# Copying softmax probabilities into float32r tiles by DMA before their transposes, and products of 128 columns in place of tiles of zeros

## The chip, the cores and the metric

The kernel runs on one core of one Trainium2 chip. Its time is the device time in microseconds (us) of one execution; three runs of the kernel before gave a median of 1428.13 us (1425.39 to 1431.31). PE is the matrix engine, DVE the vector engine, ACT the scalar engine, POOL the general-purpose engine, SP the engine that issues most DMAs. All engines run their own lists of instructions in a fixed order and wait for each other through semaphores.

## The reference, cut to what matters

One decoder layer with three branches. The change lies in the two attention branches, which have the same core; branch B is dense and causal:

```
# 8 heads, 1024 queries and keys, blocks of 128 queries
sc = einsum('bqhd,bkhd->bhqk', q, k).astype(float32) * d ** -0.5
sc = where(key_pos <= q_pos, sc, -1e30)
p  = softmax(sc, axis=-1)
o  = einsum('bhqk,bkhd->bqhd', p, v)
```

Branch A has the same products, with a mask that keeps 256 chosen keys for each query. The rest of the layer (norms, the large projections, the choice of the 256 keys, gates, the output projection) is not changed.

## The kernel before, in words

All large products are made from float32r operands: a value x is split into a high part, x copied to a tile of type float32r (which changes its last bits), and a low part, x minus the high part. A product of two split operands is two or three products.

`attention` (quoted at the end of this section) runs over 32 units for each branch: 8 heads, and within a head four pairs of query blocks G in the order 3, 0, 2, 1. A unit has two query blocks, b = 0 and b = 1, with (2G+1)*128 and (2G+2)*128 keys. For each block `Scores.mm` makes the scores on PE (tiles `b_3S`, lines 997 to 999: three products for each stretch of at most 512 keys), `masked` negates them into SBUF and takes the row's extreme on DVE (line 494), `Scores.exp` takes the exponential on ACT (line 513), and `Scores.norm` multiplies by one over the sum on DVE (line 523). The result is the tile `b_3p`: plain float32, queries on partitions, keys along the row.

`PV` then needs the probabilities with the keys on partitions. `PV.pt(kp)` transposes, on PE (line 466, into the PSUM tile `b_3pt`), the 128x128 pieces of two key blocks and two query blocks; ACT copies the four pieces into a float32r tile `th` (line 468), DVE forms the low part `tl` (line 469). `PV.mmv(kp)` makes four products with V (lines 479 and 480, tile `b_3o`): two key blocks, each times `th` and times `tl`, 256 columns wide. In the last pair of key blocks the piece (later keys, earlier queries) is masked entirely. Before, it is a strip of zeros in a fixed tile (`zt`), so that the products keep 256 columns. In the same way a score product for 128 keys is made 256 columns wide (`s_chunks`).

Between these steps PE has other work: `kv_gen` (tiles `kv`) and `k_prep` (`bkt`, line 967) prepare the next heads, `q_prep` (`b_0q`, line 979) transposes the next queries, and `Filler` makes gate products (tile `f`, lines 277 to 279, 128x512), whose weights SP loads in halves (`f_1_0r`, line 393) into a pool of `FW` split tiles. Branch B takes eight column blocks of such filler, 384 products. The code gives an order; a scheduler that plans the whole program then moves instructions of each engine, filler above all, into places where it expects the engine to wait. So the order on each engine is not that of the code, but it is fixed when the kernel is built.

In branch A the queries are already transposed as float32r (line 1465, with the float32r unit matrix `identr`); the probabilities of both branches are transposed as float32 with `ident`.

Heads are numbered 0 to 7 below, and "a G = 3 unit" is the unit with the last 256 queries of a head, the longest one.

Of the kernel before, what the change touches and what calls it, by code (L numbers as in the profile page):

```python
# [21 lines left out]
S = 1024  # L22
# [11 lines left out]
FW = 6  # L34
# [39 lines left out]
ZTB = 2  # L74
PVB = (2, 2)
PVA = (2, 2)
# [33 lines left out]
def hybrid_kernel(  # L110
# [70 lines left out]
    # rotary tables: cos / sin of f32(position) * f32(inv_freq), by token block  # L181
# [40 lines left out]
    # DRAM scratch  # L222
# [30 lines left out]
    def wload(pool, nm, srcs, a, n):  # L253
        """srcs: list of ([128, a, w] DRAM view, w); -> (hi, lo) [P, a, n]"""
# [26 lines left out]
    def proj_w(nm, pool, w, cols, nk, per=None):  # L281
        """cols: list of (c0, n) -> one (hi, lo) for each 128 rows"""
# [9 lines left out]
    def proj(nm, ks, lhs, tbs, chunks, consume):  # L292
        """out[tok, cols]; chunks: list of (off, n) within the columns"""
# [118 lines left out]
    def s_chunks(n):  # L412
        """(first key, width of the product, width used) of each bank"""
        if n <= 512:
            return [(0, max(n, 256), n)]
# [17 lines left out]
    zt = []  # L433
    zcount = [0]
    pv_bufs = [2, 2]

    def zero_tiles(wk, n):
        zt[:] = [[wk.tile([P, 4, P], FR, name=f"zt{i}{j}", bufs=1) for j in range(2)] for i in range(n)]
        for t2 in zt:
            for t in t2:  # L440
                nc.gpsimd.memset(t[:, 0, :].bitcast(F32), 0.0)

    class PV:
        """P of two query blocks (2G, 2G + 1) times V, transposed; vst(kt): [128, 128], high and low
        parts of V, the high part where the head's rows of the result lie."""

        def __init__(self, nm, wk, G, sc, hh, vst, o_dst, done):
            self.nm, self.wk, self.nk, self.Pt, self.vst, self.o_dst, self.done = nm, wk, G + 1, sc.Pt, vst, o_dst, done
            self.hh = hh
# [3 lines left out]
        def pt(self, kp):  # L453
            nm, wk, Pt = self.nm, self.wk, self.Pt
            tp = ps_t(f"{nm}pt{kp}").rearrange("p (a c) -> p a c", a=4)
            last = kp == self.nk - 1
            if last:
                th, tl = zt[zcount[0] % len(zt)]
                zcount[0] += 1
                order = [(1, 2 * kp + 1, 1), (2, 2 * kp, 0), (3, 2 * kp, 1)]  # L460
            else:
                th = wk.tile([P, 4, P], FR, tag="pth", name=f"{nm}th{kp}", bufs=pv_bufs[0])
                tl = wk.tile([P, 4, P], FR, tag="ptl", name=f"{nm}tl{kp}", bufs=pv_bufs[0])
                order = [(2 * a + b, 2 * kp + a, b) for a in range(2) for b in range(2)]
# [5 lines left out]
            kts = (2 * kp + 1, 2 * kp) if last else (2 * kp, 2 * kp + 1)  # L470
            self.t[kp] = (th.rearrange("p (a b) c -> p a (b c)", a=2), tl.rearrange("p (a b) c -> p a (b c)", a=2), kts)

        def mmv(self, kp):
            if self.o2 is None:
                self.o2 = ps_mm(f"{self.nm}o2")
            th, tl, kts = self.t.pop(kp)
# [15 lines left out]
    def masked(pt, sp, m, mask, k0, mx, c):  # L492
        """-(scores + mask), and its least value"""
# [8 lines left out]
    class Scores:  # L502
        def __init__(self, nm, wk, G, mm):
            self.nm, self.wk, self.G, self._mm = nm, wk, G, mm
            self.rs = sm.tile([P, 2], F32, tag="rsb", name=nm + "rs")
            self.Pt = []
# [10 lines left out]
        def norm(self):  # L517
            ri = sm.tile([P, 2], F32, tag="rib", name=self.nm + "ri")
            nc.vector.reciprocal(ri, self.rs)
            for b in range(2):  # L520
# [3 lines left out]
                                  scalar2=None, op0=ALU.mult)  # L524

# [3 lines left out]
    def p_tile(wk, G, nm):  # L529
        if G >= 2:  # L530
            return wk.tile([P, S], F32, tag="ptA", name=nm)
        return wk.tile([P, 512], F32, tag="ptB", name=nm)

    def attention(gen, k_prep, q_prep, scores, pv, fill, per, pre, GEN):
        """Head pairs; the next pair's operands are made between the units of this one."""
# [21 lines left out]
        def fl(k):  # L557
            """work of the next pair, then gate products"""
# [54 lines left out]
    # ================= memory branch =================  # L613
# [984 lines left out]
```

## Time and profile before

| | |
|---|---|
| runs of the kernel before | 1428.13 us, median of 3 (1425.39 to 1431.31) |
| the profiled execution | span 1427.6 us from its first to its last instruction |
| PE busy in the span | 1366.2 us (96%) |
| PE weight loads | 1173.0 us (82%) |
| DVE, ACT, POOL | 967.5 us (68%), 687.7 us (48%), 270.2 us (19%) |
| share of the last chain | PE 68%, DVE 15%, ACT 6%, issue 4%, DMA 4% |
| branch B, attention | 285 to 526 us |
| branch A, attention | 955 to 1255 us |

The page gives no other time for the profiled execution than its span. The span lies 0.5 us below the median of the runs. PE bounds most of the kernel: the 40 slices show it at eight or nine tenths nearly everywhere. Matmuls are pipelined and their rows overlap, so what one costs PE is the distance from its start to the next start, not its length.

### The profile page before, as it was taken

The numbers are of one execution on the slowest core, as the hardware profiler recorded it, in microseconds if no ns is written. First come the engines' busy times: TensorE is split into PE (matmuls) and PEld (weight loads), VectorE is DVE, ScalarE is ACT, GpSimd is POOL, SyncE is SP. The second block draws the span as 40 slices with busy tenths as digits, with TensorE's granted clock in tenths as the row PEclk, the third lists the DMA queues.
The fourth block names the chain that finished last, engine by engine and source line by source line (L and its number), as shares of the span: only waits on it lengthen the run. The fifth ranks groups of instructions, "written<-read, shape, count | busy, mean of one in ns | idle before, by whom it ended". The sixth has DMA issues, their size and how long they took to land.

```text
span 1427.6 us, 20798 instructions
## 1 busy us (share of the span) xinstructions
PE 1366.2 (96%) x7440; PEld 1173.0 (82%) x7440; DVE 967.5 (68%) x2409; ACT 687.7 (48%) x1488; POOL 270.2 (19%) x254
## 2 busy tenths in 40 slices
PE   7999999999999999898988998899999999999998
PEld 5998888888888889786867886689899898877887
DVE  5935446678888861479879678777777868836511
ACT  6635433356666651464576563224555535633200
POOL 3150003511102000200232335331202011003200
PEclk9999999999999999999998999999999999999999
DMA  7411222311111120210224325630201001185622
GB/s 245 136 45 52 78 59 86 114 56 41 49 56 53 45 93 20 67 45 23 89 79 151 97 75 182 193 85 9 67 23 45 31 15 45 38 276 184 210 96 74
DMA packets 124631, 122.34 MB, mean 86 GB/s; under 512 B 20336, under 2 KB 90224, under 8 KB 124528
## 3 DMA queue, kind: packets, MB, share of 16 engines
q1 hardware_dynamic: 123952, 118.92, 26.8%
q10 hardware_dynamic: 576, 2.10, 0.4%
q8 instruction: 58, 0.95, 0.3%
q14 instruction: 45, 0.37, 0.1%
HBM read 87.93 MB, written 33.06 MB: 85 GB/s over the span
## 4 chain that ended last, share of the span: by engine, by line
PE 68%; DVE 15%; ACT 6%; issue 4%; DMA 4%; POOL 1%; SPq 1%; ACTq 0%; DVEq 0%; POOLq 0%
PE f L277 5%; PE f L278 5%; PE f L279 4%; DVE kdj L1039 3%; PE a L277 3%; PE a L278 3%; PE a L279 3%; PE o L277 2%; PE o L278 2%; PE o L279 2%; ACT kag L1049 2%; PE br L277 2%; PE br L278 2%; PE br L279 2%; DVE sz L1292 1%
## 5 line engine op out<-in xcount | busy, mean ns | idle before, releaser
L1049 ACT ACTIVATE kag<-idx,kaT 128x512 bf16<-128x512 f32 (+2 forms) x96 | 82.9, 864 | 56.0 <-DVE kaT L1077 39.4
L277 PE MATMUL f<-hTh,f_0h 128*128 128x512 f32 x184 | 77.0, 419 | 1.9 <-ACT f_0h L248 1.2
L277 PE MATMUL f<-hTh,f_1h 128*128 128x512 f32 x184 | 75.6, 411 | 1.3 <-ACT f_1h L248 1.3
L279 PE MATMUL f<-hTh,f_0l 128*128 128x512 f32 x184 | 74.4, 405 | 0.6 <-POOL f_0l L251 0.6
L278 PE MATMUL f<-hTl,f_0h 128*128 128x512 f32 x184 | 74.5, 405 | 0.0
L279 PE MATMUL f<-hTh,f_1l 128*128 128x512 f32 x184 | 74.0, 402 | 0.0
L278 PE MATMUL f<-hTl,f_1h 128*128 128x512 f32 x184 | 73.6, 400 | 0.0
L1568 DVE TENSOR_TENSOR xr<-o,xr 128x512 f32<-128x512 f32 x16 | 11.1, 691 | 64.0 <-PE o L279 64.0
L1223 ACT ACTIVATE irl<-is 128x512 f32<-128x512 f32 (+1 forms) x80 | 37.6, 524 | 24.2 <-DVE idx L1229 15.5
L1526 POOL TENSOR_TENSOR ac<-ac,tg 128x512 f32<-128x512 f32 x16 | 23.5, 1469 | 128.6 <-DMA wo_3r<-in_w_out_dram 109.9
L1039 DVE TENSOR_SCALAR_CACHE_REDUCE kdj<-kdh,kdT 128x384 bf16<-128x384 bf16 (+2 forms) x48 | 46.3, 965 | 0.8
L1039 DVE TENSOR_SCALAR_CACHE_REDUCE kdj<-idx,kdT 128x384 bf16<-128x384 f32 (+2 forms) x48 | 46.2, 963 | 0.6
L369 ACT ACTIVATE fo<-f 128x512 f32<-128x512 f32 x48 | 28.7, 599 | 35.2 <-PE f L279 29.0
L279 PEld LDWEIGHTS f<-hTh,f_0l 128*128 128x128 f32 x184 | 35.2, 191 | 7.9 <-POOL f_0l L251 1.1
L1229 DVE SCALAR_TENSOR_TENSOR idx<-irl,wi,idx 128x1024 f32<-128x1024 f32 (+5 forms) x42 | 40.6, 966 | 1.5 <-ACT irl L1223 0.4
L277 PEld LDWEIGHTS f<-hTh,f_0h 128*128 128x128 f32 x184 | 35.1, 191 | 7.2 <-ACT f_0h L248 1.4
L279 PEld LDWEIGHTS f<-hTh,f_1l 128*128 128x128 f32 x184 | 34.8, 189 | 7.0 <-DVE f_1l L251 0.6
L277 PEld LDWEIGHTS f<-hTh,f_1h 128*128 128x128 f32 x184 | 35.0, 190 | 6.7 <-ACT f_1h L248 2.1
L278 PEld LDWEIGHTS f<-hTl,f_1h 128*128 128x128 f32 x184 | 34.9, 190 | 5.2
L278 PEld LDWEIGHTS f<-hTl,f_0h 128*128 128x128 f32 x184 | 35.3, 192 | 4.3
L1412 ACT ACTIVATE asq<-a 128x256 f32<-128x256 f32 x32 | 12.3, 384 | 51.1 <-PE a L279 50.9
L1266 DVE SCALAR_TENSOR_TENSOR sz<-sz,z 128x512 f32<-128x512 f32 x24 | 16.4, 683 | 27.7 <-ACT sz L1265 27.7
(1215 smaller groups left out, 4862.1 us busy)
## 6 DMA issues: line engine op xcount, KB each, us to landing
s_tg<-fo SPq DMA_DIRECT2D x48, 256.0 KB, 2.0
tg<-s_tg SPq DMA_DIRECT2D x48, 256.0 KB, 3.0
f_0r<-in_w_in_dram SPq DMA_DIRECT2D x23, 256.0 KB, 3.0
f_1r<-in_w_in_dram SPq DMA_DIRECT2D x23, 256.0 KB, 2.9
xx<-in_x_dram SPq DMA_DIRECT2D x8, 512.0 KB, 7.3
osb<-s_o SPq DMA_DIRECT2D x8, 512.0 KB, 3.8
s_acc<-acc SPq DMA_DIRECT2D x16, 256.0 KB, 2.4
ac<-s_acc SPq DMA_DIRECT2D x16, 256.0 KB, 3.4
```

The source lines that it names most:

```text
L277: nc.tensor.matmul(ps, ah, bh, start=start, stop=False)
L278: nc.tensor.matmul(ps, ah, bl, start=False, stop=False)
L279: nc.tensor.matmul(ps, al, bh, start=False, stop=stop)
L369: nc.scalar.activation(o, ps, AF.Tanh, scale=0.5)
L1039: nc.vector.tensor_scalar(out=junk, in0=src[t], scalar1=T[:, i:i + 1], scalar2=0.0, op0=op, op1=ALU.add, accum_out=cnt[:, i:i + 1])
L1049: nc.scalar.activation(junk, idx[t], AF.Sign, bias=T[:, i:i + 1], accum_out=cnt[:, i:i + 1])
L1223: nc.scalar.activation(rl[:, k0:k0 + m], sp[:, 0:m], AF.Relu)
L1229: i_ = nc.vector.scalar_tensor_tensor(out=acc[:, 0:n], in0=rl[:, 0:n], scalar=wc, in1=acc[:, 0:n], op0=ALU.mult, op1=ALU.add)
L1266: zi[0] = nc.vector.scalar_tensor_tensor(out=sz, in0=sz, scalar=1.0, in1=pz[j], op0=ALU.add, op1=ALU.mult)
L1292: i_ = (nc.gpsimd if n and PMUL else nc.vector).tensor_tensor(sz, osb[:, cs], sz, op=ALU.mult)
L1412: nc.scalar.activation(sq.rearrange("p h d -> p (h d)"), ps[:, 0:256], AF.Square)
L1526: nc.gpsimd.tensor_tensor(ac, ac, tg, op=ALU.add)
```

## The change

For branch B alone each normalised tile of probabilities is copied by an SP DMA, SBUF to SBUF, into a second tile whose type is float32r (`b_3r`); the DMA sees both as float32 and moves the words as they are. The transposes then read that tile, with `identr`, into a PSUM tile of type float32r. In both branches the last pair of key blocks has three pieces instead of four, and its second pair of products has 128 columns; the tiles of zeros go, and a score product for 128 keys has 128 columns. To make room, the filler's pool has 5 tiles instead of 6 and branch B's `o2s` one buffer instead of two; branch A's `th` and `tl` have three buffers instead of two. The remaining lines of the diff take comments away.

```diff
-FW = 6
+FW = 5
...
-ZTB = 2
-PVB = (2, 2)
-PVA = (2, 2)
+PVB = (2, 1)
+PVA = (3, 2)
...
         if n <= 512:
-            return [(0, max(n, 256), n)]
+            return [(0, n, n)]
...
         def pt(self, kp):
             nm, wk, Pt = self.nm, self.wk, self.Pt
-            tp = ps_t(f"{nm}pt{kp}").rearrange("p (a c) -> p a c", a=4)
+            Pr = self.Pr
+            tp = ps_t(f"{nm}pt{kp}", FR if Pr else F32).rearrange("p (a c) -> p a c", a=4)
             last = kp == self.nk - 1
-            if last:
-                th, tl = zt[zcount[0] % len(zt)]
-                zcount[0] += 1
-                order = [(1, 2 * kp + 1, 1), (2, 2 * kp, 0), (3, 2 * kp, 1)]
-            else:
...
-            for i, kt, b in order:
-                nc.tensor.transpose(tp[:, i, :], Pt[b][:, kt * P:(kt + 1) * P], ident)
-            v = slice(1 if last else 0, 4)
-            nc.scalar.copy(th[:, v, :], tp[:, v, :])
-            nc.vector.tensor_tensor(tl[:, v, :], tp[:, v, :], f(th[:, v, :]), op=ALU.subtract)
+            th = wk.tile([P, 4, P], FR, tag="pth", name=f"{nm}th{kp}", bufs=pv_bufs[0])
+            tl = wk.tile([P, 4, P], FR, tag="ptl", name=f"{nm}tl{kp}", bufs=pv_bufs[0])
+            order = [(2 * kp + a, b) for a in range(2) for b in range(2) if not (last and a > b)]
+            v = len(order)
+            for i, (kt, b) in enumerate(order):
+                ks = slice(kt * P, (kt + 1) * P)
+                if Pr:
+                    nc.tensor.transpose(tp[:, i, :], Pr[b][:, ks], identr)
+                else:
+                    nc.tensor.transpose(tp[:, i, :], Pt[b][:, ks], ident)
+            tp = f(tp) if Pr else tp
+            nc.scalar.copy(th[:, 0:v, :], tp[:, 0:v, :])
+            nc.vector.tensor_tensor(tl[:, 0:v, :], tp[:, 0:v, :], f(th[:, 0:v, :]), op=ALU.subtract)
...
         def mmv(self, kp):
...
+            last = kp == self.nk - 1
             for a in range(2):
-                vs = self.vst(kts[a])
-                nc.tensor.matmul(self.o2[:, 0:256], vs, th[:, a], start=(kp == 0 and a == 0), stop=False)
-                nc.tensor.matmul(self.o2[:, 0:256], vs, tl[:, a], start=False,
-                                 stop=(kp == self.nk - 1 and a == 1))
+                vs = self.vst(2 * kp + a)
+                o = slice(P, 256) if last and a else slice(0, 256)
+                c = slice(256 * a, 256 * a + o.stop - o.start)
+                nc.tensor.matmul(self.o2[:, o], vs, th[:, c], start=(kp == 0 and a == 0), stop=False)
+                nc.tensor.matmul(self.o2[:, o], vs, tl[:, c], start=False, stop=bool(last and a))
...
         def norm(self):
...
+                if self.hop:
+                    pr = p_tile(self.wk, self.G, f"{self.nm}r{b}", FR, "r")
+                    nc.sync.dma_start(pr[:, 0:n].bitcast(F32), self.Pt[b][:, 0:n])
+                    self.Pr.append(pr)
...
-        zero_tiles(wk, ZTB)
...
-            u = Scores(f"b{2 * p + hh}_{G}", wk, G, s_mm)
+            u = Scores(f"b{2 * p + hh}_{G}", wk, G, s_mm, True)
...
-        zero_tiles(wk2, 1)
```

The change moves instructions on every engine, as the scheduler plans anew. Three places matter for the prediction. The first is PE in branch B just ahead of the transposes of a G = 3 unit (`b_3pt`) in the middle of the branch; `f` is filler, `b_0S` the scores of the next unit, `b_1o` the products with V of the unit before. Before the change:

```order
L277 MATMUL f_1_0_4770<-hTh_0_109,f_1_0h 128x512
L278 MATMUL f_1_0_4770<-hTl_0_125,f_1_0h 128x512
L279 MATMUL f_1_0_4770<-hTh_0_109,f_1_0l 128x512
L479 MATMUL b_1o_4740<-zt_2864,vst_3312 128x256
L480 MATMUL b_1o_4740<-zt_2865,vst_3312 128x256
L479 MATMUL b_1o_4740<-zt_2864,vst_3312 128x256
L480 MATMUL b_1o_4740<-zt_2865,vst_3312 128x256
L997 MATMUL b_0S_0_4791<-bkh_4638,b_0qh 128x256
L998 MATMUL b_0S_0_4791<-bkl_4639,b_0qh 128x256
L466 MATMUL b_3pt_4796<-ident,b_3p_4694 128x128
```

In the changed kernel, the same place of the program (PE, G = 3 unit; `b_3r_4827` is the copy of block b = 0, `b_3r_4830` that of b = 1):

```order
L278 MATMUL f_2_0_5458<-hTh_0_115,f_2_0l 128x512
L276 MATMUL f_2_0_5458<-hTh_0_117,f_2_1h 128x512
L457 MATMUL b_3pt_4888<-identr,b_3r_4827 128x128
L457 MATMUL b_3pt_4905<-identr,b_3r_4827 128x128
L457 MATMUL b_3pt_4923<-identr,b_3r_4827 128x128
L277 MATMUL f_2_0_5458<-hTl_0_133,f_2_1h 128x512
L278 MATMUL f_2_0_5458<-hTh_0_117,f_2_1l 128x512
L276 MATMUL f_2_0_5458<-hTh_0_119,f_2_1h 128x512
L277 MATMUL f_2_0_5458<-hTl_0_135,f_2_1h 128x512
L278 MATMUL f_2_0_5458<-hTh_0_119,f_2_1l 128x512
L457 MATMUL b_3pt_4888<-identr,b_3r_4830 128x128
```

More filler stands ahead of the transposes, and the pieces of block b = 0 go first, with five more filler products between them and the first piece of b = 1. Over the whole list of the changed kernel, the first seven G = 3 units and the first six G = 2 units of branch B have such filler (or `kv`) products ahead of their transposes; the last G = 3 unit and the last two G = 2 units have none.

The second place is PE at the end of branch B, from the last score product of the last G = 2 unit on. Before the change:

```order
L999 MATMUL b_2S_1_6024<-bkh_5539,b_2ql 128x256
L277 MATMUL f_3_1_6009<-hTh_1_110,f_3_0h 128x512
L278 MATMUL f_3_1_6009<-hTl_1_126,f_3_0h 128x512
L279 MATMUL f_3_1_6009<-hTh_1_110,f_3_0l 128x512
L277 MATMUL f_3_1_6009<-hTh_1_112,f_3_0h 128x512
L278 MATMUL f_3_1_6009<-hTl_1_128,f_3_0h 128x512
L279 MATMUL f_3_1_6009<-hTh_1_112,f_3_0l 128x512
L277 MATMUL f_3_1_6009<-hTh_1_114,f_3_1h 128x512
L278 MATMUL f_3_1_6009<-hTl_1_130,f_3_1h 128x512
L279 MATMUL f_3_1_6009<-hTh_1_114,f_3_1l 128x512
L479 MATMUL b_0o_6051<-zt_2864,vst_4920 128x256
L480 MATMUL b_0o_6051<-zt_2865,vst_4920 128x256
```

And in the changed kernel, PE from the same score product to the first transpose of that unit (`b_2pt`):

```order
L998 MATMUL b_2S_1_6196<-bkh_5679,b_2ql 128x256
L474 MATMUL b_0o_6227<-b_0th_6174,vst_5024 128x256
L475 MATMUL b_0o_6227<-b_0tl_6175,vst_5024 128x256
L474 MATMUL b_0o_6227<-b_0th_6174,vst_5024 128x128
L475 MATMUL b_0o_6227<-b_0tl_6175,vst_5024 128x128
L996 MATMUL b_1S_0_6238<-bkh_5679,b_1qh 128x384
L997 MATMUL b_1S_0_6238<-bkl_5680,b_1qh 128x384
L996 MATMUL b_1S_0_6255<-bkh_5679,b_1qh 128x512
L997 MATMUL b_1S_0_6255<-bkl_5680,b_1qh 128x512
L998 MATMUL b_1S_0_6238<-bkh_5679,b_1ql 128x384
L998 MATMUL b_1S_0_6255<-bkh_5679,b_1ql 128x512
L457 MATMUL b_2pt_6243<-identr,b_2r_6206 128x128
```

The filler products are gone from here: they now stand in the heads before. Of branch B's filler one half block (`f_4_1`, 24 products) is left, and it stands behind all attention work of the branch. The third place is the queue of SP in the middle of branch B, where `s_tg` are stores of finished gates, `f_1_0r` and the like weight loads of the filler, `xqp` the queries of the next head. Before the change:

```order
L370 DMA s_tg_102<-fo_7_0_3872 128x512
L393 DMA f_1_0r<-in_w_in_dram 128x4x128
L961 DMA xqp_4636<-s_qb 128x8x96
L370 DMA s_tg_102<-fo_7_1_4205 128x512
L393 DMA f_1_1r<-in_w_in_dram 128x4x128
L370 DMA s_tg_101<-fo_0_0_4494 128x512
```

In the changed kernel, SP's queue there, with the copies of line 523:

```order
L369 DMA s_tg_102<-fo_7_1_4261 128x512
L392 DMA f_1_0r<-in_w_in_dram 128x4x128
L523 DMA b_3r_3969<-b_3p_3922 128x896
L523 DMA b_3r_3972<-b_3p_3945 128x1024
L523 DMA b_0r_4060<-b_0p_4024 128x128
L523 DMA b_0r_4063<-b_0p_4041 128x256
L369 DMA s_tg_101<-fo_0_0_4568 128x512
L960 DMA xqp_4722<-s_qb 128x8x96
L523 DMA b_2r_4158<-b_2p_4120 128x640
L523 DMA b_2r_4161<-b_2p_4142 128x768
L392 DMA f_1_1r<-in_w_in_dram 128x4x128
```

There are 64 copies, two for each unit, and each stands in the queue at the place where the plan has its normalisation end.

## Rows read from the trace of the kernel before

**Rows 1.** Stages: us, busy of PE, PEld, DVE, ACT, POOL (count), PEclk, DMA share, GB/s

```profile
285.00:526.00 241.00, 237.70 (x1492) 207.10 (x1493) 198.59 (x582) 152.00 (x367) 25.58 (x29) 0.99 0.17 52
...
955.00:1255.00 300.00, 293.71 (x1785) 265.44 (x1785) 233.07 (x724) 156.45 (x368) 39.04 (x32) 0.99 0.14 41
```

**Rows 2.** Waits of PE in 285 to 526 us: total, times, longest

```profile
PE bkt L967 <- POOL xk L952: 2.4, 1, 2.4
PE b_3S L997 <- DVE b_3mx L494: 0.4, 2, 0.2
```

**Rows 3.** Line 466, branch B: duration ns min/median/max, first and last start

```profile
L466 PE MATMUL b_3pt<-ident,b_3p x120: 270/272/328, 302.6 to 506.6; 128*128 128x128 f32 x120
...
L466 PE MATMUL b_2pt<-ident,b_2p x88: 270/272/323, 314.2 to 516.8; 128*128 128x128 f32 x88
...
L466 PE MATMUL b_1pt<-ident,b_1p x56: 270/272/274, 325.1 to 521.2; 128*128 128x128 f32 x56
...
L466 PE MATMUL b_0pt<-ident,b_0p x24: 270/272/273, 309.2 to 510.0; 128*128 128x128 f32 x24
```

**Rows 4.** Line 1465, float32r transposes of branch A: weight load, matmul

```profile
L1465 PEld LDWEIGHTS a_2q<-identr,a_2qs x16: 138/141/143, 976.7 to 1233.8; 128*128 128x128 f32 x16
L1465 PE MATMUL a_2q<-identr,a_2qs x16: 218/226/228, 976.8 to 1233.9; 128*128 128x128 f32 x16
```

**Rows 5.** Timeline of PE, 302 to 307 us: start, length, instruction, count

```profile
302.08 0.40 PE L279 MATMUL f<-hTh,f_0l 128*128 128x512 f32 x1
302.32 0.40 PE L277 MATMUL f<-hTh,f_1h 128*128 128x512 f32 x1
302.55 0.49 PE L466 MATMUL b_3pt<-ident,b_3p 128*128 128x128 f32 x3
...
306.35 0.28 PE L480 MATMUL b_3o<-b_3tl,vst 128*128 128x256 f32 x1
306.47 0.29 PE L479 MATMUL b_3o<-b_3th,vst 128*128 128x256 f32 x1
```

**Rows 6.** Timeline of PE in branch A, two float32r transposes

```profile
1233.80 0.29 PE L1465 MATMUL a_2q<-identr,a_2qs 128*128 128x128 f32 x2
```

**Rows 7.** Line 479, products with a tile of zeros: weight load, matmul

```profile
L479 PEld LDWEIGHTS b_0o<-zt,vst x16: 187/188/192, 319.4 to 513.8; 128*128 128x128 f32 x16
L479 PE MATMUL b_0o<-zt,vst x16: 276/282/363, 319.4 to 514.0; 128*128 128x256 f32 x16
```

**Rows 8.** DMA issues: count, KB each, median us from issue to landing

```profile
s_tg<-fo SPq DMA_DIRECT2D x48, 256.0 KB, 2.0
...
osb<-s_o SPq DMA_DIRECT2D x8, 512.0 KB, 3.8
...
s_qb<-xqb SPq DMA_DIRECT2D x8, 384.0 KB, 2.4
...
s_o<-ob ACTq DMA_DIRECT2D x4, 512.0 KB, 2.7
```

**Rows 9.** Timeline of PE: the last score product of three units

```profile
310.87 0.28 PE L999 MATMUL b_2S<-bkh,b_2ql 96*128 96x256 f32 x1
...
385.70 0.39 PE L999 MATMUL b_3S<-bkh,b_3ql 96*128 96x512 f32 x1
...
413.20 0.39 PE L999 MATMUL b_3S<-bkh,b_3ql 96*128 96x512 f32 x1
```

**Rows 10.** Timeline of DVE: the normalisations of the same three units

```profile
313.57 1.08 DVE L523 TENSOR_SCALAR b_2p<-b_2p,b_2ri 128x640 f32<-128x640 f32 x2
...
388.69 1.35 DVE L523 TENSOR_SCALAR b_3p<-b_3p,b_3ri 128x896 f32<-128x896 f32 x2
...
416.98 1.35 DVE L523 TENSOR_SCALAR b_3p<-b_3p,b_3ri 128x896 f32<-128x896 f32 x2
```

**Rows 11.** Stages around the one long wait of PE in branch B

```profile
283.00:287.30 4.30, 1.87 (x13) 1.52 (x12) 3.62 (x13) 1.85 (x6) 3.98 (x4) 1.00 0.20 67
...
288.70:292.20 3.50, 3.50 (x10) 2.70 (x9) 2.83 (x6) 1.01 (x3) 0.56 (x1) 0.51 0.04 12
```

More of the change, by code (lines that the diff above doesn't have):

```diff
@@ L431, in rope @@
         nc.vector.tensor_tensor(x2, tt[2], tt[3], op=ALU.add)
-    zt = []
-    zcount = [0]
     pv_bufs = [2, 2]
[L437 to L441, printed above, removed]
     class PV:
@@ L448, in __init__ @@
             self.nm, self.wk, self.nk, self.Pt, self.vst, self.o_dst, self.done = nm, wk, G + 1, sc.Pt, vst, o_dst, done
-            self.hh = hh
+            self.hh, self.Pr = hh, sc.Pr
             self.t = {}
@@ L454, in pt @@
             nm, wk, Pt = self.nm, self.wk, self.Pt
-            tp = ps_t(f"{nm}pt{kp}").rearrange("p (a c) -> p a c", a=4)
+            Pr = self.Pr
+            tp = ps_t(f"{nm}pt{kp}", FR if Pr else F32).rearrange("p (a c) -> p a c", a=4)
             last = kp == self.nk - 1
-            if last:
-                th, tl = zt[zcount[0] % len(zt)]
-                zcount[0] += 1
-                order = [(1, 2 * kp + 1, 1), (2, 2 * kp, 0), (3, 2 * kp, 1)]
-            else:
-                th = wk.tile([P, 4, P], FR, tag="pth", name=f"{nm}th{kp}", bufs=pv_bufs[0])
-                tl = wk.tile([P, 4, P], FR, tag="ptl", name=f"{nm}tl{kp}", bufs=pv_bufs[0])
-                order = [(2 * a + b, 2 * kp + a, b) for a in range(2) for b in range(2)]
-            for i, kt, b in order:
-                nc.tensor.transpose(tp[:, i, :], Pt[b][:, kt * P:(kt + 1) * P], ident)
-            v = slice(1 if last else 0, 4)
-            nc.scalar.copy(th[:, v, :], tp[:, v, :])
-            nc.vector.tensor_tensor(tl[:, v, :], tp[:, v, :], f(th[:, v, :]), op=ALU.subtract)
-            kts = (2 * kp + 1, 2 * kp) if last else (2 * kp, 2 * kp + 1)
-            self.t[kp] = (th.rearrange("p (a b) c -> p a (b c)", a=2), tl.rearrange("p (a b) c -> p a (b c)", a=2), kts)
+            th = wk.tile([P, 4, P], FR, tag="pth", name=f"{nm}th{kp}", bufs=pv_bufs[0])
[11 more added lines that the diff above has]
+            nc.vector.tensor_tensor(tl[:, 0:v, :], tp[:, 0:v, :], f(th[:, 0:v, :]), op=ALU.subtract)
+            self.t[kp] = (th.rearrange("p i c -> p (i c)"), tl.rearrange("p i c -> p (i c)"))
         def mmv(self, kp):
@@ L475, in mmv @@
                 self.o2 = ps_mm(f"{self.nm}o2")
[L476 removed]
+            th, tl = self.t.pop(kp)
+            last = kp == self.nk - 1
             for a in range(2):
[L478 to L481 removed]
+                vs = self.vst(2 * kp + a)
[3 more added lines that the diff above has]
+                nc.tensor.matmul(self.o2[:, o], vs, tl[:, c], start=False, stop=bool(last and a))
         def evac(self):
@@ L502, in hybrid_kernel, with __init__ @@
     class Scores:
-        def __init__(self, nm, wk, G, mm):
+        def __init__(self, nm, wk, G, mm, hop=False):
             self.nm, self.wk, self.G, self._mm = nm, wk, G, mm
+            self.hop, self.Pr = hop, []
             self.rs = sm.tile([P, 2], F32, tag="rsb", name=nm + "rs")
@@ L524, in norm, with p_tile @@
                                   scalar2=None, op0=ALU.mult)
+                if self.hop:
+                    pr = p_tile(self.wk, self.G, f"{self.nm}r{b}", FR, "r")
+                    nc.sync.dma_start(pr[:, 0:n].bitcast(F32), self.Pt[b][:, 0:n])
+                    self.Pr.append(pr)
     GORD = (3, 0, 2, 1)
     KP1 = 0
-    def p_tile(wk, G, nm):
+    def p_tile(wk, G, nm, dt=F32, kind=""):
         if G >= 2:
-            return wk.tile([P, S], F32, tag="ptA", name=nm)
-        return wk.tile([P, 512], F32, tag="ptB", name=nm)
+            return wk.tile([P, S], dt, tag="ptA" + kind, name=nm)
+        return wk.tile([P, 512], dt, tag="ptB" + kind, name=nm)
     def attention(gen, k_prep, q_prep, scores, pv, fill, per, pre, GEN):
```

## Prediction

> **What bounds the kernel now.** I read the stages first. Attention of branch B takes 241 us and that of branch A 300 us, and PE is busy for 237.7 and 293.7 of them, at a granted clock of 0.99, the higher of its two levels [rows 1]. DVE is next in branch B with 198.6 us. Then I read PE's waits in branch B: one of 2.4 us, and next to nothing besides [rows 2]. So in both branches an instruction taken off PE is worth its time, as long as PE is not made to wait instead. The change does both: it shortens PE's work, and in branch B it puts a DMA between the normalisation and the transposes.
>
> **Transposes as float32r.** Branch B has 120 + 88 + 56 + 24 = 288 of them [rows 3]. Three in a row last 0.49 us, one 0.272, so they start (0.49 - 0.272) / 2 = 0.109 us apart [rows 3, 5]. Float32r transposes of the same shape are in branch A: two last 0.29 us, one 0.226, so 0.06 us apart [rows 4, 6]. The saving is 288 x 0.048 = 13.8 us of PE. I see no reason why a copied tile should be transposed otherwise than branch A's queries, so this term has no wide range.
>
> **Products of 128 columns.** Each of the 64 units loses 128 columns in two products, and the scores for 128 keys in three products of eight units in branch B and two of eight in branch A: 64 x 2 + 24 + 16 = 168 products. The 256-column ones start 0.12 us apart, 512-column ones 0.23 to 0.24 [rows 5], so at first sight 128 columns cost 0.06, as the float32r transposes do: -168 x 0.058 = -9.7 us. That is one end. But no row shows a float32r product, other than a transpose, of fewer than 256 columns. The weight load of a product takes 188 ns and that of a float32r transpose 141 [rows 4, 7]: 47 ns longer, where transposes follow each other every 60. If loads set the pace, a product can't start more often than every 0.06 + 0.047 = 0.107 us, however narrow, and 168 x 0.012 = 2.0 us are saved. The other end: float32 transposes take nearly twice the time of float32r ones with the same columns, so the engine has slower ways through its columns; were narrow products streamed four times, they would cost as much as 512 columns, 0.231, and 168 x 0.111 = 18.6 us would be lost. I take -2.0, since the two weight-load rows are the nearest to the case.
>
> The Trainium skill, page "TensorE: Matmul & The Clock Gate", section "LDWEIGHTS (loading the stationary operand)", speaks against the narrow products: a load takes its number of columns over 1.2 GHz, which for 128 is 107 ns (an estimate by that page). The product's weight load agrees with that, the transpose's doesn't, as it keeps a pace of 60 ns. By the page alone the narrow products would save those same 2 us, and the float32r transposes next to nothing; for the latter the rows decide.
>
> **The copies.** Rows of SBUF-to-SBUF copies don't exist here. Stores out of SBUF land 2.0, 2.4 and 2.7 us after issue for 256, 384 and 512 KB, loads of 512 KB after 3.8 [rows 8]; so 1.3 us plus 0.7 for each 256 KB, or up to a microsecond more. A G = 3 unit has copies of 448 and 512 KB, the second issued 0.75 us after the first. If they share the engines, the second lands 1.3 + 0.7 x 960 / 256 - 0.75 = 3.2 us after the second normalisation; a G = 2 unit (320 and 384 KB) 1.3 + 0.7 x 704 / 256 - 0.6 = 2.6 us. I take these, for the stores read SBUF as the copies do. The ends are 2.0 (each for itself, as a small store) and 4.2 and 3.6.
>
> Before, the way from the last score product to the end of the second normalisation took 416.98 + 1.35 - 413.20 = 5.1 us for one G = 3 unit and 4.3 for the shortest, and 3.8 for a short G = 2 unit [rows 9, 10]. PE had to have work for that long. Now it has to have it for 7.5 to 8.3 us and 6.4 us.
>
> In the new order I counted what stands between, by the spacings above (512 columns 0.231, 384 0.175, 256 0.119, narrow products 0.107). In the first seven G = 3 units this is 6.2 to 7.2 us up to the first transpose of block 0, whose copy is needed about 1.4 us earlier than that of block 1, and 7.7 to 8.4 us up to the first of block 1. In the first six G = 2 units it is 7.1 to 7.8 us for block 1. So there the copies are just covered; I allow 0.2 us for each G = 3 unit, 1.5 us in all. G = 0 and G = 1 units have 6.5 us and more, ample for small copies.
>
> The cover is filler, and it is used up. Ahead of the last two G = 2 units' transposes stand only the products of the neighbours: 2 x 0.119 + 2 x 0.107 for V, 3 x 0.175 + 3 x 0.231 for scores, 0.119 for the last score product itself: 1.8 us, and 2.0 to block 1. Needed are 6.4. PE waits 4.4 us, twice. Ahead of the last G = 3 unit stand 2.1 to 2.3 us against 7.5: 5.2 us. Together 14.0 us. The half block of filler behind the branch can't help, as it is queued after them.
>
> **The clock.** The one long wait of branch B (2.45 us within the first stretch) was followed by 3.5 us at a granted clock of 0.51, the lower level [rows 11], where work takes twice its time: 1.7 us lost. Three waits of 4 to 5 us can do this three times; some of that work lies in front of another wait, so I take 4 us, between 0 and 5.
>
> **What else moves.** SP gets 64 issues, and a copy at its head holds up the weight loads and stores behind it until DVE has normalised. The filler's weights then come later, with one buffer less; the plan counts on that, and 0 is my value. If a store of a gate stands ahead of a copy and is late, the copy is late: up to 0.5 us in some units, within the range. ACT and DVE keep their evictions, 512 or 384 columns as before. DMA shares of 0.17 in branch B leave room for 19 MB more. POOL loses six memsets outside PE's path.
>
> **The sum.** -13.8 - 2.0 + 1.5 + 14.0 + 4 = +3.7 us on the profiled 1427.6 us, 1431.3; the median of the runs lies 0.5 us above the span, so 1432 us.
>
> **Rivals.** (a) Everything cheap: narrow products at 0.06 us and copies that land after 2.0 us. Then -13.8 - 9.7, nothing in the covered units, 2 x 3.8 + 4.1 = 11.7 at the end and 2 us of clock: -9.8, 1418 us. The transposes' pace speaks for it, the longer weight load against it. (b) Slower: narrow products pass four times. Then 18.6 us are lost where I count a gain of 2.0; the wider products cover 0.3 us more of each long wait, so the sum is 3.7 + 20.6 - 1 = +23, 1451 us. It decides from about 0.15 us a product on, where the term turns from 0 to +5. Against it stands the float32r transposes' pace at 128 columns; for it, that no row excludes it. (c) Slower through the copies: 4.2 and 3.6 us. Then the covered units wait too, seven times 1.2 and six times 0.5 us, and the end 3 us longer: 14.4 us more, less the 1.5 allowed there, so +16.6 in all, 1445 us. Loads of 512 KB at 3.8 us speak for it, stores at 2.7 against.
>
> **How the numbers follow.** A change of under 0.5%, 7 us, can't be told from none here. Forecast 0.5 (its own range 1424 to 1439), (a) 0.15, (b) 0.2, (c) 0.15. Of the forecast I give 0.1 below 1421 us and 0.25 above 1435; of (a) 0.75 is faster, the rest is no change; (b) and (c) are nearly all slower. Faster: 0.05 + 0.11 = 0.16. Slower: 0.13 + 0.20 + 0.13 = 0.46, of which I move 0.04 to no change as the last waits may be shorter than bounded. Same: 0.42. The range from 1418 to 1452 us takes in (c), the middle of (a) and the middle of (b).
>
> **What would show it.** Right: transposes of branch B about 0.06 us apart; three idle stretches of PE of 4 to 5 us at the end of branch B, ended by the copies or the transposes' wait for them, with half the clock after each; branch B as long as before within a few us; filler products ahead of the transposes and hardly a wait in the first six heads. Wrong: 128-column products 0.2 us apart would show (b), 0.06 (a). Waits of over a microsecond in early G = 3 units would show that the copies take longer than the stores.

## The result, and the profile after

The changed kernel takes 1479.88 us (median of four runs, 1476.65 to 1483.23), 1.0362 times the kernel before, interval 1.034 to 1.0385: 52 us slower. The forecast was 1432, its range ended at 1452. Branch B, from its first transpose of keys to the first product of the next stage, went from 246.4 to 283.3 us (gate products left over at its end are in this length); branch A, from its first transpose of keys to the end of its last product with V, from 296.8 to 306.6.

The page shows more PE busy than before (1366.2 us), though its work became less, and a notch in the clock, in branch B, that was not there:

```profile
PE 1383.7 (94%) x7440; PEld 1178.1 (80%) x7440; DVE 965.4 (65%) x2409; ACT 687.4 (47%) x1488; POOL 269.2 (18%) x248
...
PEclk9999999999999988999999999999999999999999
```

Stages of after, in the columns of [rows 1]: the two branches, and three stretches at the end of branch B:

```profile
285.00:566.00 281.00, 252.92 (x1506) 211.44 (x1507) 198.02 (x582) 154.03 (x368) 26.08 (x29) 0.95 0.33 114
995.00:1295.00 300.00, 288.45 (x1733) 259.43 (x1732) 228.35 (x712) 151.97 (x363) 36.24 (x30) 0.98 0.12 34
...
523.00:530.00 7.00, 5.24 (x24) 4.50 (x25) 2.28 (x5) 1.92 (x4) 0.00 (x0) 0.51 0.41 155
...
540.00:547.00 7.00, 5.64 (x28) 5.02 (x29) 2.42 (x4) 2.24 (x5) 0.00 (x0) 0.51 0.27 97
553.00:564.00 11.00, 6.43 (x31) 5.50 (x31) 5.29 (x14) 3.97 (x10) 0.00 (x0) 0.54 0.60 217
```

DVE and ACT have about as much to do as before; PE has waits. Those of branch B, beside [rows 2]:

```profile
PE b_2pt L457 <- DMA b_2r<-b_2p: 9.3, 4, 4.3
PE f L276 <- ACT fo L368: 7.7, 7, 2.2
PE b_3pt L457 <- DMA b_3r<-b_3p: 6.0, 3, 4.5
PE bkt L966 <- POOL xk L951: 2.4, 1, 2.4
```

Seven waits for the copies hold 15.3 us, and a second kind, which the forecast didn't have, 7.7: a gate block waits until ScalarE has read the block before it out of the one PSUM bank they share. The timeline of PE in after shows the first end wait and the pace of what follows:

```profile
519.34 0.57 PE L998 MATMUL b_1S<-bkh,b_1ql 96*128 96x384 f32 x2
524.19 0.59 PE L457 MATMUL b_2pt<-identr,b_2r 128*128 128x128 f32 x3 [4.28 <-DMA b_2r<-b_2p]
525.16 1.25 PE L457 MATMUL b_2pt<-identr,b_2r 128*128 128x128 f32 x8 [0.38 <-DMA b_2r<-b_2p]
...
530.14 0.28 PE L475 MATMUL b_2o<-b_2tl,vst 128*128 128x256 f32 x1
530.26 0.22 PE L474 MATMUL b_2o<-b_2th,vst 128*128 128x128 f32 x1
530.32 0.28 PE L475 MATMUL b_2o<-b_2tl,vst 128*128 128x128 f32 x1
530.43 0.44 PE L998 MATMUL b_3S<-bkh,b_3ql 96*128 96x512 f32 x1
...
531.24 0.46 PE L457 MATMUL b_1pt<-identr,b_1r 128*128 128x128 f32 x4
```

PE stands for 4.28 us, then works at half the clock (0.51 above, the lower of its two levels) until about 530. At full clock again, four float32r transposes take 0.46 us; with 0.22 for one that is 0.08 us from start to start, not 0.06. Two narrow products start 0.06 apart, and the next instruction only 0.11 later: 0.17 us for a pair that took 0.24. The two other end waits:

```profile
540.52 0.59 PE L457 MATMUL b_3pt<-identr,b_3r 128*128 128x128 f32 x3 [4.46 <-DMA b_3r<-b_3p]
...
557.00 0.59 PE L457 MATMUL b_2pt<-identr,b_2r 128*128 128x128 f32 x3 [4.27 <-DMA b_2r<-b_2p]
```

### The profile page after: what moved, and what is told of

It reads as the page before. It is cut to its first block, busy times and chain, and to the rows that moved or that the text cites. A ratio compares the mean times of both kernels' runs of the same rounds, so it can differ in the third digit from the quotient of the medians.

```text
span 1476.5 us, 21084 instructions
## 1 busy us (share of the span) xinstructions
PE 1383.7 (94%) x7440; PEld 1178.1 (80%) x7440; DVE 965.4 (65%) x2409; ACT 687.4 (47%) x1488; POOL 269.2 (18%) x248
## 4 chain that ended last, share of the span: by engine, by line
PE 65%; DVE 16%; ACT 6%; DMA 5%; issue 4%; POOL 1%; SPq 0%; ACTq 0%; DVEq 0%; POOLq 0%
PE f L276 5%; PE f L277 4%; PE f L278 4%; PE a L276 3%; PE a L277 3%; PE a L278 3%; DVE kdj L1038 3%; PE o L276 2%; PE o L278 2%; PE o L277 2%; ACT kag L1048 2%; PE br L277 2%; PE br L276 2%; PE br L278 2%; DVE idx L1228 1%
## 5 line engine op out<-in xcount | busy, mean ns | idle before, releaser
L1222 ACT ACTIVATE irl<-is 128x512 f32<-128x512 f32 (+1 forms) x80 | 38.0, 525 | 23.6 <-DVE idx L1228 13.1
L462 DVE TENSOR_TENSOR b_3tl<-b_3pt,b_3th 128x512 fp32r<-128x512 f32 (+1 forms) x32 | 20.2, 655 | 29.0 <-ACT b_3th L461 29.0
L1410 ACT ACTIVATE asq<-a 128x256 f32<-128x256 f32 x32 | 12.3, 385 | 56.1 <-PE a L278 56.0
```

The lines of the kernel that those rows point to most:

```text
L462: nc.vector.tensor_tensor(tl[:, 0:v, :], tp[:, 0:v, :], f(th[:, 0:v, :]), op=ALU.subtract)
L1222: nc.scalar.activation(rl[:, k0:k0 + m], sp[:, 0:m], AF.Relu)
L1410: nc.scalar.activation(sq.rearrange("p h d -> p (h d)"), ps[:, 0:256], AF.Square)
```

## The experiments

The kernel before, timed beside them, had medians of 1427.3 to 1428.5 us. B and A are the stage lengths defined above, from each profile.

| run | us | ratio, 95% interval | B | A |
|---|---|---|---|---|
| before | 1428 | | 246.4 | 296.8 |
| after | 1479.9 | 1.0362 (1.0340 to 1.0385) | 283.3 | 306.6 |
| e1 no copy, float32 transposes | 1446.2 | 1.0127 (1.0110 to 1.0143) | 252.1 | 307.7 |
| e2 normalisation writes float32r | 1443.5 | 1.0109 (1.0093 to 1.0125) | 249.2 | 307.8 |
| e3 copies in six heads | 1462.4 | 1.0244 (1.0224 to 1.0264) | 269.6 | 305.7 |
| e4 copies from GpSimd's queue | 1496.8 | 1.0477 (1.0452 to 1.0502) | 303.0 | 305.6 |
| f1 narrow products alone | 1440.4 | 1.0090 (1.0075 to 1.0105) | 250.0 | 306.7 |
| f2 short rings alone | 1429.6 | 1.0015 (1.0005 to 1.0024) | 245.0 | 299.4 |
| f3 more gate products in B | 1490.5 | 1.0434 (1.0416 to 1.0451) | 310.7 | 305.6 |
| f4 narrow, three tiles a ring | 1440.0 | 1.0096 (1.0080 to 1.0113) | 251.3 | 308.0 |
| g1 narrow scores alone | 1430.4 | 1.0028 (1.0017 to 1.0039) | 248.3 | 297.3 |
| g2 narrow V products alone | 1441.4 | 1.0108 (1.0085 to 1.0131) | 248.5 | 308.9 |
| g3 two banks for gate products | 1491.0 | 1.0453 (1.0436 to 1.0471) | 289.2 | 310.1 |
| g5 float32r, no low part | 1409.9 | 0.9879 (0.9852 to 0.9905) | 224.7 | 297.2 |
| i1 narrow V, own tiles | 1439.3 | 1.0077 (1.0056 to 1.0097) | 250.9 | 306.4 |
| i2 wide, no tiles of zeros | 1434.7 | 1.0040 (1.0025 to 1.0055) | 246.1 | 301.3 |
| j1 as i2, with copies | 1477.8 | 1.0345 (1.0323 to 1.0367) | 289.4 | 301.1 |
| j2 as i2, writing float32r | 1431.7 | 1.0024 (1.0014 to 1.0034) | 242.8 | 301.3 |
| k1 narrow V, A's heads 0 to 4 | 1428.2 | 1.0001 (0.9990 to 1.0013) | 246.4 | 298.6 |
| k2 narrow V, A's heads 5 to 7 | 1432.1 | 1.0026 (1.0012 to 1.0039) | 244.9 | 302.9 |

B and A come from one profile each. In before, f2 and g5 PE has the same order in branch A, and A is 296.8, 299.4 and 297.2 us: a difference of 2.6 us in A can come from the execution alone.

**The copies away, and the float32r transposes without them.** e1 and e2, from after; e2 rounds branch B's probabilities to float32r:

```
e1: scores(): Scores(..., s_mm, True) -> Scores(..., s_mm, False)
e2: norm():  eng.tensor_scalar(out=pr[:, 0:n], in0=Pt[b][:, 0:n], ...)   # pr is the float32r tile, no dma_start
```

> The changed kernel without the copies: branch B transposes its probabilities as float32 again, all else of the change stays (128-column products in both branches, no tiles of zeros, 5 filler tiles, one o2s buffer, three th/tl buffers in branch A). Theory C (the copies and what they make the plan do cost the time): the loss goes, and the narrow products save what the trace of the changed kernel shows, a pair 60 + 110 ns instead of 2 x 119, 84 pairs, about 6 us: 1418 to 1430 us. Theory N (narrow products or the buffers cost it): 1460 us or more.

> The changed kernel with the copy left out in another way: the normalisation on DVE writes its product straight into the float32r tile, so the low bits of the probabilities are dropped there (this kernel computes them less exactly), and the transposes are float32r as in the change. Theory C: no latency between normalisation and transposes, so no waits at the end of branch B; the transposes save 288 x 25 to 48 ns against e1_no_copy: 1408 to 1424 us. Theory T (float32r transposes themselves bring the loss, through their weight loads or the clock): near the changed kernel, 1465 us or more.

Neither theory had it. The copies with the float32r transposes cost 34 us, but 18 remain without them; branch A, where there are no copies, is 11 longer in the profile. And float32r transposes without the copy (e2 against e1) give 2.7 us, not 14.

**Which heads pay for the copies.** e3 leaves the copies out in heads 6 and 7 (`True` becomes `p < 3`), e4 issues them from GpSimd's queue:

> The copies only in heads 0 to 5; heads 6 and 7 transpose float32 as before. Theory E (most of the loss is at the end of branch B, where the filler is used up: three waits of 4.3 us and the half clock after them): the waits shrink to about 1 us each, 20 to 25 us come back: 1455 to 1462 us. Theory M (the loss is spread over all heads with copies): a quarter of the 52 us goes, 1467 us, in proportion to two heads of eight.

> The same copies, issued from POOL's queue instead of SP's. Theory Q (a copy at the head of SP's queue holds up gate stores and filler weights, and the filler's first products then wait): the eight waits of filler for ACT's gate function in branch B (7.7 us) go, 10 us or more come back: below 1470 us. Theory C without Q: the waits at the end of branch B stay, and the time stays within 8 us of the changed kernel's 1480.

e3 gives 17.5 us back, less than the 20 to 25 of theory E and more than the 13 of theory M. Its longest waits of PE in branch B (those for `b_2p` are in heads 6 and 7):

```profile
PE f L276 <- ACT fo L368: 7.7, 7, 2.2
PE b_2pt L459 <- DVE b_2p L518: 2.9, 2, 1.8
...
PE b_3pt L457 <- DMA b_3r<-b_3p: 0.8, 1, 0.8
```

Almost nothing is waited for a copy there (0.8 us): the cover holds, as forecast. It is bought with gate blocks laid end to end, and these wait for each other. It is also taken from heads 6 and 7. The gate products alone, in heads 0 to 5 and then in heads 6 and 7 (a head ends with its last product with V); the columns are the length, PE, PEld and ACT, then clock and DMA. First e1, then e3, then the second stretch of after:

```profile
287.50:482.10 194.60, 70.39 (x246) 43.83 (x246) 5.99 (x10) 0.99 0.17 48
482.10:530.70 48.60, 21.07 (x73) 12.66 (x74) 1.79 (x3) 1.00 0.20 56
...
286.80:504.10 217.30, 92.71 (x314) 57.84 (x315) 7.70 (x13) 0.98 0.35 116
504.10:551.40 47.30, 7.09 (x23) 3.62 (x23) 0.60 (x1) 0.96 0.14 43
...
504.40:565.60 61.20, 6.05 (x23) 3.78 (x24) 0.60 (x1) 0.80 0.30 110
```

PE's other products in these stretches are the same in number, to within two. In heads 0 to 5, e3 has 68 gate products more than e1; at 0.231 us each they are 15.7 of the 22.7 us by which these heads are longer, and 7.0 are lost. In heads 6 and 7 it has 50 fewer, 11.6 us of work, and is only 1.3 us shorter: 10 us are lost where no copy stands and the gate products are missing. In after the same two heads lose 24 (61.2 - 48.6 + 11.6).

In e4 the copies leave SP's queue free but come later: PE waits 16.4 and 14.2 us for them. Its gate blocks wait 3.0 us for each other instead of 7.7, yet the time is 17 us above after's, outside both forecasts. So SP as the cause was not supported; what a free SP alone would give wasn't separated from the slower queue.

```profile
PE b_2pt L457 <- DMA b_2r<-b_2p: 16.4, 9, 4.9
PE b_3pt L457 <- DMA b_3r<-b_3p: 14.2, 7, 5.1
```

**More cover.** f3 moves two of the three gate jobs of the next stage into branch B (`NFB` 8 to 10, `NFI` 3 to 1); g3 gives the gate products of branch B a second kind of PSUM bank (`'f'` to `'fm'`; branch A's gate products take their banks from the same entry, so they change too); both from after:

> The changed kernel whole, with ten gate jobs instead of eight in branch B and one instead of three in the indexer: the same gate products, more of them where the copies are waited for. Theory F (the copies cost because the gate products run out, so that the last three waits of 4.3 us stand open and the clock halves behind them): those three waits and their half clock, about 25 us, go, the indexer loses some cover, and the time is 1450 to 1466 us. Rival G (the gate products are only moved from a place where they hide as much): 1475 to 1490 us.

> The changed kernel whole, with the gate products of branch B in two PSUM banks in turn instead of one. In the changed kernel PE waits 7.7 us in seven places at the start of a gate block until ScalarE has read the block before it, since the scheduler lays gate blocks end to end to cover the copies. Theory K (this is a cost of its own, apart from the copies' landing): the 7.7 us and the half clock after the longest of them, 1.7 us, go, and the time is 1465 to 1473 us. Rival (the cover is then used up sooner, or the waits move to the transposes): 1476 to 1484 us.

Theory F fell; f3's time lies where the range of rival G ends. But f3 was no test of more cover. It moves 96 products, 96 x 0.231 = 22 us, and the next stage is 11 us shorter, branch B 27 longer. Yet the plan laid them behind all attention work of the branch: 116 gate products stand there (first line), 22 in after (second line).

```profile
569.60:598.10 28.50, 27.44 (x116) 21.20 (x116) 2.39 (x4) 1.00 0.40 125
...
565.70:570.60 4.90, 4.90 (x22) 3.79 (x21) 0.00 (x0) 1.00 0.27 107
```

Of the 27 us 23.6 are these products, and only 3.8 lie in the attention itself (282.1 against 278.3 us). About 2 us of products stand ahead of the transposes of the last G = 3 and G = 2 units, as in after, and the waits stay:

```profile
PE b_2pt L457 <- DMA b_2r<-b_2p: 10.2, 5, 4.3
...
PE b_3pt L457 <- DMA b_3r<-b_3p: 5.9, 3, 4.4
```

Whether gate products ahead of the last units would take these waits away was not tested. g3 missed both its forecasts: branch B is 5.9 us longer than in after, branch A 3.5. The gate blocks' waits in branch B are gone, and others stand there:

```profile
PE b_2pt L457 <- DMA b_2r<-b_2p: 9.2, 4, 4.3
PE b_3pt L457 <- DMA b_3r<-b_3p: 7.4, 5, 4.6
PE b_1S L996 <- ACT b_1qh L981: 3.8, 2, 1.9
```

The added banks are those that `kv` and the products with V use; that these came to wait for them is my reading, and not shown.

**The 18 us without copies.** f1 takes after's narrow products alone, with the rings of before; f2 is before with `FW` 5 and `PVB` (2, 1); f4 is f1 with three tiles `th` and `tl`:

> The narrow products and the layout without tiles of zeros alone: no copies, fp32 transposes, and the rings of the kernel before (six weight tiles for the gate products, two output tiles and two of each part of the transposed probabilities). The kernel without copies stood at 1446 us, 18 above before. Theory R (the shorter rings made those 18): 1420 to 1431 us here. Rival N (the narrow products, or the order that the work falls into without the tiles of zeros, made them): 1438 to 1448 us, and branch A, whose rings are the only other thing that differs there, 8 us or more longer than before.

> The kernel before with the two shorter rings of branch B (five weight tiles for the gate products instead of six, one output tile instead of two) and nothing else: products of 256 columns, tiles of zeros, fp32 transposes, no copies. Theory R: 1436 to 1447 us. Rival N: 1426 to 1432 us.

> As the narrow products alone, with three instead of two tiles of each part of the transposed probabilities in both branches (before, the tiles of zeros stood beside the two and took the last part of each unit). Theory R2 (these two tiles are the short ring): 4 us or more below the narrow products alone. Otherwise within 3 us of it.

Rival N holds: 13 us come with the narrow products and the layout without tiles of zeros, 2 with the rings, and a longer ring does nothing. g1 is before with `(0, n, n)` in `s_chunks`, g2 is f1 with `max(n, 256)` back:

> The kernel before with score products of 128 columns where 128 keys are wanted, and nothing else: 40 products fewer columns, tiles of zeros and their products as before. Narrow products alone cost 13 us; theory V (that lies in the products with V and in what stood around the tiles of zeros): 1426 to 1431 us here. Rival O (any product that the scheduler counts as shorter moves its order, and the cost is that of a worse order, not of one kind of product): 1433 to 1440 us.

> The narrow products alone, but with score products of at least 256 columns again: 128 columns in the last pair of products with V, no tiles of zeros, rings and transposes as before. Theory V: 1436 to 1443 us, as with all the narrow products (1440). Rival O: between 1430 and 1437 us, the rest of the 13 us being with the scores.

It is the products with V: narrow scores alone cost 3 us, and nothing beside them (g2 is no shorter than f1). i1, from g2, gives the last pair tiles of its own again; i2, from before, keeps products of 256 columns and takes the tiles of zeros away:

```
i1: th = wk.tile(..., tag="pth" + ("z" if last else ""), bufs=pv_bufs[2 if last else 0])   # tl alike
i2: if last: for t in (th, tl): nc.gpsimd.memset(t[:, 0, :].bitcast(F32), 0.0)
```

> Narrow products with V as in the kernel that has these alone (1441 us), but the last pair of each unit has tiles of its own again, two of each part in branch B and one in branch A, as the tiles of zeros were. Theory T (the last pair now waits for a tile that the pair before it still uses; the width is harmless): 1426 to 1432 us. Rival W (the width of the products, or the order and the cover that come with it, costs): 1437 to 1444 us.

> The other half: the kernel before with its products of 256 columns, but without fixed tiles of zeros; the last pair takes a tile of the common ring, and GpSimd writes the strip of zeros into it each time (two small writes for each of 64 units, off PE's path). Theory T: 1436 to 1444 us. Rival W: 1426 to 1432 us.

With tiles of its own the last pair still costs 11 us (i1), so their loss is not the cause. With wide products it costs some 7 us (i2, between its two forecasts; GpSimd also writes the zeros for each unit there), 4.5 of it in branch A. k1 and k2 change nothing but the width, in some heads of branch A of the kernel before:

```
nar = last and self.nm[0] == "a" and int(self.nm[1]) in range(5)     # k2: range(5, 8)
for i, a in enumerate((1, 0) if nar else (0, 1)):
    o = slice(P, 256) if nar and i else slice(0, 256)                # o2[:, o], th[:, a, o], tl[:, a, o]
```

> The kernel before with the last products with V 128 columns wide (the second query block's half alone) in heads 0 to 4 of branch A and nowhere else; tiles of zeros, rings and transposes stay. Branch B's order on PE is the same as before, and so is that of branch A's last heads. 40 units' halves of products, 40 products, become narrow. Theory L (a narrow product saves a little, and what costs 10 us in branch A is the order of its last three heads, where the gate products that cover the softmax run thin): branch A 295 to 298 us (before 296.8), the whole 1425 to 1430 us. Rival E (narrow products cost wherever they stand): branch A 301 to 304 us, the whole 1432 to 1436 us.

> The same in heads 5 to 7 of branch A alone, 24 products, everything before them in the order of the kernel before. Theory L: branch A 302 to 307 us, the whole 1433 to 1438 us, with new waits in the last heads. Rival E: branch A 299 to 301 us, the whole 1430 to 1433 us.

40 narrow products in the early heads cost nothing that can be measured, as theory L has it and theory E hasn't. 24 in the late ones cost 3.6 us in the runs (0.0026 of 1428), which is beyond the noise. The time of 1432.1 is below theory L's 1433 and in theory E's range, while branch A's 302.9 is in theory L's. In k2's profile 3.3 of branch A's 6.1 us lie in heads 5 to 7; the rest lies in heads 0 to 4, where PE has the order of before. Branch A's waits of PE for the next scores in k1, then the longest in k2:

```profile
PE a_1S L1483 <- DVE a_1qT L1469: 0.9, 3, 0.4
...
PE a_2S L1483 <- DVE a_2mx L496: 0.6, 2, 0.4
```

```profile
PE a_2S L1483 <- DVE a_2mx L496: 3.3, 2, 2.9
```

A score product of G = 2 in head 5 now stands for 2.9 us behind VectorE, at a place where before has no such wait. The trace shows why. VectorE's own order changed: in before (first two lines) it reads the scores and then takes up `axq`, which comes from GpSimd; in k2 (third line) and in after (fourth) `axq` stands first, and VectorE waits for GpSimd with the scores unread.

```profile
1184.31 0.56 DVE L494 CUSTOM_DVE_ANT_0 a_2p<-a_2S,msk 128x384 f32<-128x384 f32 x1
...
1187.47 0.22 DVE L426 TENSOR_TENSOR ar_1rp<-axq,cos_a 128x64 f32<-128x64 f32 x1
...
1185.73 0.23 DVE L426 TENSOR_TENSOR ar_1rp<-axq,cos_a 128x64 f32<-128x64 f32 x1 [2.77 <-POOL axq L1432]
...
1228.28 0.23 DVE L425 TENSOR_TENSOR ar_1rp<-axq,cos_a 128x64 f32<-128x64 f32 x1 [2.78 <-POOL axq L1428]
```

After has the same wait of PE, and one of a gate block:

```profile
PE a_2S L1479 <- DVE a_2mx L488: 2.9, 1, 2.9
...
PE f L276 <- ACT fo L368: 1.8, 1, 1.8
```

f1 doesn't have it, though its branch A is as long as after's, and 8.5 of its 9.9 us lie in heads 0 to 4. So the late heads are not the whole of it.

**Copies and transposes with wide products.** j1 is i2 with the copies and after's rings in branch B; j2 is j1 with the normalisation writing the float32r tile, rounded, and no copy:

> The changed kernel's copies and float32r transposes in branch B, with its shorter rings there, but with products of 256 columns everywhere (strip of zeros written by GpSimd, as above). If the narrow products and the copies simply add up, 14 us come off the changed kernel's 1480: 1463 to 1470 us. Rival (the copies' waits fill what the narrow products leave, in branch B at least, so that only branch A's 10 us come off, and the gate products run out one unit earlier, a fourth wait of 4 us): 1471 to 1478 us.

> As the one with wide products and copies, but VectorE's normalisation of branch B writes the float32r tile itself (rounded) and there is no copy: what the float32r transposes are worth by themselves. 288 x 0.025 us = 7 us below wide products with float32 transposes, and 2 us above for the shorter rings: 1420 to 1426 us. Rival (the shorter transposes take away as much cover as they save): 1427 to 1434 us.

The parts don't add up: with copies, wide products save 2 us, not 14; the time is in the rival's range. Branch A is 5.5 us shorter, branch B 6.1 longer. The fourth long wait of the rival didn't come, but the cover runs out sooner: j1 has 333 gate products in heads 0 to 5 and 3 in heads 6 and 7, after 314 and 22. So the copies with their transposes cost 34 us beside narrow products and 43 beside wide ones (j1 against i2, 41 without the rings' 2). j2 against i2 says again that float32r transposes are worth 3 us (about 5, if the rings' 2 us are counted); the rival's range, 1427 to 1434, holds the time.

**A version that beats both.** Where the normalisation writes float32r, the low part is zero, so g5 leaves it out in branch B (from before, wide products, short rings):

```
eng.tensor_scalar(out=pr[:, 0:n], ...)                       # pr float32r; transposes with identr
# no tensor_tensor(tl, ...); one product with V for each key block: matmul(o2, vs, th[:, a])
```

> The kernel before with VectorE's normalisation of branch B writing the float32r tile itself, no copy, float32r transposes, and, since the low part of such a value is zero, no low part: no subtraction and 160 products with V fewer in branch B. The probabilities of branch B are so rounded to float32r, which before they were not. Products and tiles of zeros stay as before, the two rings of branch B are the shorter ones (alone 1429.6 us). If PE's work is the bound: 160 x 0.128 + 288 x 0.025 = 27.7 us less, 1400 to 1408 us. If the shorter cover opens waits for the softmax instead (rival): half of it is lost, 1412 to 1424 us.

1409.9 us, 17 below the before timed beside it and between the two forecasts; branch B is 20.3 us shorter than in f2, of 27.7 counted. PE is still its bound:

```profile
286.00:512.00 226.00, 222.70 (x1369) 190.14 (x1370) 159.84 (x501) 152.59 (x370) 24.39 (x27) 0.99 0.21 62
```

It is a different trade: branch B's probabilities carry float32r's bits and no more.

## Why the prediction was wrong, step by step

Two steps failed. One is that work taken off PE is worth its time: the transposes and the narrow products stood in the sum with -15.8, and the runs have about -3 and +18 (with the rings). The other is that gate products cover the copies for next to nothing: +1.5 in the sum, where the runs show 7 us lost in heads 0 to 5, with the transposes' gain in it, and 10 more in heads 6 and 7, from which the gate products were taken.

- **Transposes, -13.8: about -3 to -5.** The pace of 0.06 us, taken from pairs, was wrong. The trace of before had longer runs of float32r transposes, in the choice of the 256 keys, which I left out:

```profile
603.92 0.46 PE L1210 MATMUL iqt<-identr,iqs 128*128 128x128 f32 x4
...
641.75 1.14 PE L1210 MATMUL iqt<-identr,iqs 128*128 128x128 f32 x12
```

  (1.14 - 0.24) / 11 = 0.082 us: only the first of a run follow at 0.06. 288 x (0.109 - 0.082) = 7.8 us was there to be had; e2 got 2.7 and j2 3 to 5. By the Trainium skill's page "TensorE: Matmul & The Clock Gate", section "LDWEIGHTS (loading the stationary operand)", which I set aside for this term, the load of 128 columns takes 107 ns (an estimate by that page); the 0.082 of the longer run lies between that and my 0.06. A rule and a row that disagree should have sent me to a third row.
- **Narrow products, -2.0: the pace was right, the sign was not.** A pair takes 0.17 us instead of 0.24, as the pace worked out from the weight-load rows says (the loads of [rows 4] and [rows 7] themselves last 141 and 188 ns); rival (b)'s four passes are out. But f1 costs 13 us. I priced instructions and not the order: a shorter product moves the scheduler's plan, in dozens of places of branch A in k1 and in k2 alike, on VectorE too. Of the two only k2 cost time. My sum has about -1 for branch A; it is 10 us longer in f1's profile, and 6.0 of them are idle time of PE, 12.3 us instead of 6.3. Before, then f1:

```profile
953.00:1249.80 296.80, 290.51 (x1774) 263.10 (x1773) 233.28 (x725) 156.20 (x369) 40.48 (x34) 0.99 0.13 38
...
952.30:1259.00 306.70, 294.35 (x1769) 263.51 (x1768) 236.78 (x725) 155.91 (x367) 40.93 (x34) 0.98 0.13 36
```

  Of the 13 us the order in the late heads has 3.6 (k2). What moves the early heads of f1, and branch B, stays open.
- **Covered units, +1.5: nothing is waited for copies there, and yet 16 us are lost** (e3 against e1, 1462.4 - 1446.2). Before the end waits the longest wait for a copy is 0.8 us, so the copies' landing was priced well. 7.0 us are lost in heads 0 to 5. By the traces PE is idle there for 9.2 us, in e1 for 4.9, the most of it gate blocks waiting for their one bank (7.7), which I had taken as free cover; with 1.7 us of half clock after the longest of these waits that is 6.1 of the 7.0. The transposes' gain of 3.4 (e2's heads 0 to 5 against e1's) should have come off and didn't: about 4 us there stay open. The other 10 of the loss lie in heads 6 and 7, which in e3 have no copies and hardly any gate products. g3 doesn't show that a second bank brings the 7.7 back.
- **Three end waits, +14.0: right.** 4.28, 4.46 and 4.27 us, 13.0 in all, where 4.4, 5.2 and 4.4 were forecast.
- **Clock, +4: about 9.** In the three stretches at half clock PE was busy 5.24 + 5.64 + 6.43 = 17.3 us, half of it lost. I took the 3.5 us after [rows 11] as the length of such a stretch; they were about 7, 7 and 10. With the waits this is 22 us, near the 24 that heads 6 and 7 of after lose; e3 gives back only 17.5 of it, as its last heads pay the float32 transposes and a wait of 1.8 for the softmax.
- **Landing of the copies: near.** 3.2 us were forecast for the 512 KB copy, the page of after has 3.5, beside 2.0 for the stores of [rows 8]. **SP's queue, 0:** open (e4 was no clean test).
- **Branch B as long as before: wrong,** 283.3 us against 246.4.

In sum, of the 48 us between forecast and time 25 come with the copies of heads 0 to 5 (three quarters of -13.8, plus 1.5, is -8.9; measured 16.2, of which 10 show in heads 6 and 7), 20 with the narrow products and rings (-2.0; e1 has 18.5), and 3 with the copies of heads 6 and 7 (a quarter of -13.8, plus 14.0 and 4, is 14.6; measured 17.5). This split takes the copies away first. Taken the other way round (i2, j1, after), the lost tiles are 7 us, the copies with the rings 43 and the narrow products 2. I think the parts overlap because both draw on the same gate products (j1 has used 19 more of them up by head 6), but no run separates it. The waits that could be counted in the order held; what I had taken for gains did not.

## What to carry to other kernels

In a kernel whose order is planned and whose engine is 96% busy, a shorter instruction is not a gain by itself: the plan moves with it, on the other engines too (here VectorE came to wait for GpSimd with PE behind it), so look for new waits before counting the gain. Take the pace of an instruction from a run as long as the new one will be, not from a pair. Cover for a latency is paid for even when it holds, since the filler is laid end to end and then waits for itself, and it is missing where it stood before.

## What the runs showed of the hardware

- Float32r transposes of 128x128: 0.06 us apart at first, 0.082 in a run of twelve; float32 ones 0.109 [rows 5].
- Two products of 128 columns with float32r weights: second start after 0.06 us, next instruction after 0.11.
- With waits of PE of 4.3 to 4.5 us, the granted clock was 0.51 over 7 us, twice, and 0.54 over 11 us a third time.
- A copy of 512 KB from SBUF to SBUF landed after 3.5 us in the median, a store of 256 KB after 2.1:

```profile
s_tg<-fo SPq DMA_DIRECT2D x48, 256.0 KB, 2.1
...
b_3r<-b_3p SPq DMA_DIRECT2D x8, 512.0 KB, 3.5
```
